# A hybrid DeltaNet and retention layer: blocks 4 and 5 of the MLP made as a pair by seven products, and the opening taken third by third

## The chip, the cores and the metric

The kernel runs on one core of a Trainium2 chip. The metric is the time of one execution on the device, in microseconds. TensorE multiplies, VectorE (DVE in the rows), ScalarE (ACT) and GpSimd (POOL) do the element work, and the queue of SyncE (SP) issues nearly all transfers. TensorE's granted clock is shown as a share of full speed (1.00 is 2.4 GHz, 0.50 is 1.2 GHz).

## The reference

One layer with two mixers beside each other and an MLP, for 128 prompt and 1024 sample tokens that share the weights. What matters here is how the layer begins and its MLP:

```python
D_MODEL = 1024; SEQ = 128; DEC_SEQ = 1024; D_FF = 4 * D_MODEL

def trunk(x, cond, ...):
    mod = jnp.einsum('bd,de->be', jax.nn.silu(cond), w_mod[l]) + b_mod[l]
    sh1, sc1, g1, sh2, sc2, g2 = jnp.split(mod[:, None, :], 6, axis=-1)
    h = layer_norm(x) * (1.0 + sc1) + sh1
    y, sd, sr = mixer(h, ...)
    x = layer_norm(ALPHA * x + g1 * y, ln1_w[l], ln1_b[l])
    h = layer_norm(x) * (1.0 + sc2) + sh2
    f = jnp.einsum('btf,fd->btd', jnp.square(jax.nn.relu(jnp.einsum('btd,df->btf', h, w_ff1[l]) + b_ff1[l])),
                   w_ff2[l]) + b_ff2[l]
    x = layer_norm(ALPHA * x + g2 * f, ln2_w[l], ln2_b[l])
```

Everything is float32.

## The kernel before, in words

The 1152 tokens lie along the free axis, and the 1024 channels on the partitions, in eight pieces k. Each float32 matrix is held as a high part (a cast by ACT, line 160 in `split`) and a low part (what is left, a subtraction by VectorE, line 161), and each product is three matmuls: high by high, low by high, high by low. The modulated, normalised input h stands in three thirds of 384 tokens, `hH[c]` and `hL[c]`.

**The opening.** `run` executes the steps of a string in order; `^n` puts a step n places ahead in the scheduler's priority. In `STA` a step `x` loads 128 tokens, `l` normalises them, `m` makes a part of the modulation vectors, and `gck` (`modulate_x`) makes the unit of third c and piece k: three transposes on TensorE (line 325), the scaling on ACT (line 328) and on VectorE or ACT (lines 333, 338), and the low part on VectorE or POOL (line 342). The first dense product (line 194) reads all eight units of a third.

**The first MLP product** follows a string `FF1`. A step `F` makes one block of 128 rows of f in the ordinary way, three thirds of 24 matmuls with 384 columns (`dense`, line 194), then relu and square on ACT (lines 1159, 1160) and a store of each third to `HR[f]`. Of F0, F1 and F2 only the first third is left here, the others having been made earlier. A step `P` (`pair`, line 1282) makes two blocks at once by seven products of half size, in the order 3, 4, 6, 7, 5, 2, 1. Each (`product`, line 1246) has two halves of 12 matmuls with 288 columns, 168 matmuls for a pair; the weights are combined by POOL (line 1302) and split; the results are added up by ACT (line 1311) and VectorE (line 1308) in two `af` buffers. Blocks 6 to 31 are the pairs P3 to P15, whose rows and sums `pair_out` stores for the second MLP product; that takes them by seven products too, and the six blocks of `HR` ordinarily.

**The operands of the seven products.** Products 2 and 5 need only copies of quarters of h (`gather`, line 1221, on ACT). Products 3, 4, 6, 7 and 1 need differences and sums of quarters. A step `S` (`combination`) makes one of them, in two halves: `combine` (line 1194) loads the two quarters' halves, 576 KB each, from `HX` in DRAM into two of three `af` buffers, adds them on VectorE (line 1200), casts the high part on ACT (line 1202) and makes the low part on VectorE (line 1203). The `Z` step (`gather_plain`) makes the copies and operand 1. What sets the order: the string sets when a step is written; the scheduler orders each engine's queue by it and by its priorities; the `af` buffers, three, set when a load may start. In the queue of SP a load that waits for its buffer holds up what is behind it.

The text names products by their number and the two halves of an operand by their columns. In rows, `sh`, `sl` are the parts of operands 3, 4, 6 and 7, `d` is an accumulator, `wh`, `wl` the parts of a weight, `rl` a third of a block.

Of the kernel before, what the change touches and what calls it, by code (L numbers as in the profile page):

```python
# [12 lines left out]
ALU = mybir.AluOpType  # L13
# [5 lines left out]
NT = 1152  # L19
# [6 lines left out]
CH = 288  # L26
STA = "x0^150 x4^1000 m2 x1^1000 x5^150 x3^50 x2^400 x6^1000 m0^50 l1 x7^50 l0^50 l2^50 x8 l3^150 l4 m3 l5 m1^1000 g01 g00 l7^1000 l6^400 l8 g02 g03 g10 g21 g12^2500 g22^2500 g11^150 g20^1000 g14^400 g13^150 g23 g06^400 g27 g17 g05^2500 g24^6000 g26^50 g15^2500 g25^150 g04 g07^50 g16^150"
RET = "V2 K0 Q0^150 Z0 V0 S0 O0 V1^400 S1^2500 D^150 N0^150 T0 O1^1000 M1 Q1 N1^2500 T1 K1 Z1^50 M2^1000 M3^50 S2 M0^50 O2^2500 V3^150 N2 S3 T2 O3^1000 N3^1000 T3^50"
DEL = "P0 i0 v0^1000 P1^50 m0^2500 G1 i1 G5 v1^150 b0 s0 P2 G6 b1^50 n0 t0^6000 m1 i2^150 v2 s1 P3 i3 n1 b2^1000 t1^2500 m2 G7 v3 s2^50 G0^150 G4 b3^2500 G2 m3 W^1000 n2 t2^150 s3^400 G3^50 n3^400 O^150 R0 t3^50 R1^1000 R2 R3 R4 R5"
OPS = "L0 M0 L1^1000 L2^400 L3^1000 M1 A0^400 A1 M2 B0^150 A2 L4^400 B1 M3 C0 M4 A3 L5 L6^50 B2 C1 M5 L7 L8 A4 M6 B3 C3 M7 C2 A5 B4 A6^400 B5 A7 M8 C4 C5 B6"  # L30
FFS = "F11 F01 A8 B7 B8^2500 F12 F02 C7 F21 C6^150 C8^6000 F22"
FF1 = "F0 S3 F1 S4 F2 S6 F3 S7 F4 F5 Z0 P3 P4 P5 P6 P7 P8 P9 P10 P11 P12 P13 P14 P15"
NEG = -1.0e30
# [47 lines left out]
def layer_kernel(ctx: ExitStack, tc: tile.TileContext, A, O):  # L81
# [202 lines left out]
    with tc.tile_pool(name="start", bufs=1) as st:  # L284
# [16 lines left out]
        p = pss()  # L301
# [891 lines left out]

    def combine(name, q, u, v, op_):

        x, y = (sb(fq, [128, NT], "af", 3).rearrange("p (k c) -> p k c", c=CH) for _ in range(2))
        for z, n in ((x, u), (y, v)):
            i, j = int(n[0]) - 1, TH * (int(n[1]) - 1) + CH * q
            dma(z, HX[512 * i:512 * i + 512, j:j + CH].rearrange("(k p) c -> p k c", p=128))
        V.tensor_tensor(out=x, in0=x, in1=y, op=op_)  # L1200
        hi, lo = (z[:, :, CH * q:CH * q + CH] for z in H[name])
        S.copy(out=hi, in_=x)
        V.tensor_tensor(out=lo, in0=x, in1=hi.bitcast(F32), op=ALU.subtract)
# [20 lines left out]
    def gather_plain():  # L1224

        q11 = gather(new_quarters(fq, "z0"), "11", 0), gather(new_quarters(hpool, "hH0"), "11", 1)
        q22 = gather(new_quarters(hpool, "hL0"), "22", 0), gather(new_quarters(hpool, "hH1"), "22", 1)
        H["2"], H["5"] = q11, q22
        H["1"] = new_quarters(hpool, "hH2"), new_quarters(hpool, "hL1")
        for q in range(2):  # L1230
            combine("1", q, "11", "22", ALU.add)

# [103 lines left out]
    def pair_stage(p):  # L1336
        rows_ = pair(p)
        if p < NP - 1:
            pair_out(*rows_)
        else:  # L1340
            last_pair.append(rows_)
# [214 lines left out]
```

## Time and profile before

| | |
|---|---|
| median of 3 runs | 1589.14 us (1587.22 to 1591.74) |
| the profiled execution | 1597.36 us |
| its span in the trace | 1595.5 us |
| TensorE busy | 1507.1 us, 94% of the span |
| VectorE, ACT, POOL busy | 1057.4, 724.6, 333.4 us |
| mean granted TensorE clock | 0.977 |
| moved by DMA | 247.81 MB |

Times in rows are microseconds from the start of the span; 1.9 us of the profiled execution lie outside it. A matmul's duration in a row overlaps with the next one's, so the cost of a matmul in a stream is the distance between starts. "Idle before" in brackets is how long the engine had stood still ahead of that instruction, and what it waited for last.

### The profile page before, as it was taken

The numbers are of one execution on the slowest core, as the hardware profiler recorded it, in microseconds if no ns is written. First come the engines' busy times: TensorE is split into PE (matmuls) and PEld (weight loads), VectorE is DVE, ScalarE is ACT, GpSimd is POOL, SyncE is SP. The second block draws the span as 40 slices with busy tenths as digits, with TensorE's granted clock in tenths as the row PEclk, the third lists the DMA queues.
The fourth block names the chain that finished last, engine by engine and source line by source line (L and its number), as shares of the span: only waits on it lengthen the run. The fifth ranks groups of instructions, "written<-read, shape, count | busy, mean of one in ns | idle before, by whom it ended". The sixth has DMA issues, their size and how long they took to land.

```text
span 1595.5 us, 26235 instructions
## 1 busy us (share of the span) xinstructions
PE 1507.1 (94%) x9597; PEld 1328.6 (83%) x9597; DVE 1057.4 (66%) x2045; ACT 724.6 (45%) x1562; POOL 333.4 (21%) x328
## 2 busy tenths in 40 slices
PE   4899999899999999999798999999999999999997
PEld 2697676898898989987687999999998788888885
DVE  4415424568795788657894576656666887867887
ACT  4522312564564464352457565445554453443411
POOL 2201021211112022100541035556553000000000
PEclk9799999999999999999898999999999999999998
DMA  9233556332323123454345944443347989878511
GB/s 347 74 82 83 172 157 200 77 78 70 82 49 102 37 58 108 122 163 161 104 152 158 292 154 139 154 155 128 125 139 260 333 281 315 290 237 284 169 54 66
DMA packets 227378, 247.81 MB, mean 155 GB/s; under 512 B 35956, under 2 KB 161889, under 8 KB 227121
## 3 DMA queue, kind: packets, MB, share of 16 engines
q1 hardware_dynamic: 227249, 246.13, 48.5%
q8 instruction: 76, 1.25, 0.3%
q14 instruction: 53, 0.43, 0.1%
HBM read 185.72 MB, written 56.15 MB: 152 GB/s over the span
## 4 chain that ended last, share of the span: by engine, by line
PE 51%; DVE 10%; issue 4%; ACT 3%; DMA 2%; POOL 2%; SPq 0%; DVEq 0%; POOLq 0%; ACTq 0%
PE d L1252 18%; PE m L1416 14%; PE mm L194 7%; PE d L194 3%; PE p L1416 2%; DVE lnst L245 2%; PE c L900 1%; PE c L891 1%; PE c L884 1%; DVE qk L638 1%; PE co L915 1%; PE co L914 1%; DVE wl L161 1%; DVE acc L1491 1%; POOL lnmv L157 1%
## 5 line engine op out<-in xcount | busy, mean ns | idle before, releaser
L194 PE MATMUL mm<-hH,wh 128*128 128x384 f32 x696 | 247.4, 356 | 2.0 <-ACT raw L634 2.0
L194 PE MATMUL mm<-hL,wh 128*128 128x384 f32 x696 | 246.6, 354 | 0.0
L194 PE MATMUL mm<-hH,wl 128*128 128x384 f32 x696 | 245.7, 354 | 0.0
L161 DVE TENSOR_TENSOR wl<-wr,wh 128x512 fp32r<-128x512 f32 (+1 forms) x149 | 126.8, 855 | 118.3 <-ACT wh L160 109.4
L1416 PE MATMUL m<-vh,sh 128*128 128x512 f32 x460 | 180.6, 393 | 3.4 <-DVE af L1308 3.0
L1416 PE MATMUL m<-vl,sh 128*128 128x512 f32 x460 | 179.8, 393 | 1.4 <-DVE vl L161 1.3
L1416 PE MATMUL m<-vh,sl 128*128 128x512 f32 x460 | 179.6, 391 | 0.4 <-DVE sl L161 0.4
L194 PEld LDWEIGHTS mm<-hH,wh 128*128 128x128 f32 x696 | 133.9, 192 | 7.3 <-ACT raw L634 2.2
L194 PEld LDWEIGHTS mm<-hL,wh 128*128 128x128 f32 x696 | 133.5, 192 | 5.5 <-issue 4.1
L194 PEld LDWEIGHTS mm<-hH,wl 128*128 128x128 f32 x696 | 133.4, 192 | 4.9 <-issue 3.7
L160 ACT CAST wh<-wr 128x512 fp32r<-128x512 f32 (+1 forms) x149 | 88.9, 613 | 78.8 <-PE mm L194 52.2
L1252 PE MATMUL d<-sh,wl 128*128 128x288 f32 x416 | 122.9, 295 | 0.5 <-DVE wl L161 0.5
L1252 PE MATMUL d<-sh,wh 128*128 128x288 f32 x416 | 122.7, 295 | 0.6 <-ACT wh L160 0.6
L1252 PE MATMUL d<-sl,wh 128*128 128x288 f32 x416 | 122.6, 295 | 0.0
L160 ACT CAST sh<-ar 128x512 fp32r<-128x512 f32 x103 | 63.8, 619 | 94.1 <-PE m L1416 46.1
L1416 PEld LDWEIGHTS m<-vh,sh 128*128 128x128 f32 x460 | 86.7, 189 | 22.9 <-issue 3.8
L157 POOL TENSOR_TENSOR lnmv<-lnmv,ex 128x1 f32<-128x1 f32 x36 | 22.0, 612 | 396.4 <-DVE lnmv L249 379.4
L1416 PEld LDWEIGHTS m<-vl,sh 128*128 128x128 f32 x460 | 86.5, 188 | 20.9 <-DVE vl L161 2.1
L1416 PEld LDWEIGHTS m<-vh,sl 128*128 128x128 f32 x460 | 86.8, 189 | 19.1 <-DVE sl L161 0.8
L161 DVE TENSOR_TENSOR sl<-ar,sh 128x512 fp32r<-128x512 f32 x103 | 70.7, 688 | 33.6 <-ACT sh L160 27.6
L1252 PE MATMUL d<-hH,wh 128*128 128x288 f32 x312 | 91.5, 294 | 0.0
L160 ACT CAST vh<-br 128x512 fp32r<-128x512 f32 x103 | 63.8, 619 | 48.9 <-DVE br L1380 32.2
(394 smaller groups left out, 3677.1 us busy)
## 6 DMA issues: line engine op xcount, KB each, us to landing
br<-in_w_ff_dram SPq DMA_DIRECT2D x168, 256.0 KB
ar<-HS SPq DMA_DIRECT2D x91, 256.0 KB
HS<-hL SPq DMA_DIRECT2D x65, 256.0 KB
wm<-in_w_mod_dram SPq DMA_DIRECT2D x32, 512.0 KB
wr<-in_w_in_dram SPq DMA_DIRECT2D x56, 256.0 KB
af<-HX SPq DMA_DIRECT2D x20, 576.0 KB
wm<-in_w_mod_dram SPq DMA_DIRECT2D x8, 1024.0 KB
w3h<-in_w_ff_dram SPq DMA_DIRECT2D x13, 512.0 KB
```

Of the source, the lines that this page charges most:

```text
L157: G.tensor_tensor(out=out, in0=in_, in1=ex[:, 0, 0:n], op=ALU.pow)
L160: S.copy(out=pool_hi, in_=src)
L161: V.tensor_tensor(out=pool_lo, in0=src, in1=pool_hi.bitcast(F32), op=ALU.subtract)
L194: T.matmul(p[:, 0:384], x[:, k % 4, :], y[c][:, k, :], start=(k == 0 and a == 0), stop=(k == 7 and a == 2),)
L245: V.bn_stats(out=st[:, j, :], in_=x[:, 512 * j:512 * j + 512])
L638: V.scalar_tensor_tensor(out=y, in0=raw[:, tap:tap + 1156], scalar=vec2[:, 12 * tap + ct:12 * tap + ct + 1], in1=y, op0=ALU.mult, op1=ALU.add,
L884: T.matmul(p[:, 0:128], qk[:, 0, off(n):off(n) + 128], old, start=True, stop=True)
L891: T.matmul(p[:, 0:128], UP[:, m_, 0, :], r, start=True, stop=True)
L900: T.matmul(p[:, 0:128], kt[:, n, :], y2, start=True, stop=True)
L914: T.matmul(p[:, 128:256], qk[:, 1, off(n):off(n) + 128], old, start=True, stop=True)
L1252: T.matmul(p[:, q, :], w[x][:, k, :], hs[y][:, k, CH * q:CH * q + CH], start=(k == 0 and a == 0), stop=(k == 3 and a == 2),)
L1416: T.matmul(p, x[i], w[j], start=(first and a == 0), stop=(last and a == 2))
```

## The change

In the opening, the units of a third are written one after another, those of the first four pieces ahead of those of the last four, and without most priorities. In the first MLP product, F4 and F5 go, and a step P2 comes behind Z: blocks 4 and 5 are made as a pair. P2 does not go through `pair_out`: its two rows are stored whole to `HR[4]` and `HR[5]`, so that the second MLP product finds its six ordinary blocks as before. Operand 1 is no longer loaded into `af` buffers but into the space of `hL2`, the low part of the last third, which is free once its last reader is done.

```diff
--- before.py
+++ after.py
@@ -24,12 +24,12 @@
-STA = "x0^150 x4^1000 m2 x1^1000 x5^150 x3^50 x2^400 x6^1000 m0^50 l1 x7^50 l0^50 l2^50 x8 l3^150 l4 m3 l5 m1^1000 g01 g00 l7^1000 l6^400 l8 g02 g03 g10 g21 g12^2500 g22^2500 g11^150 g20^1000 g14^400 g13^150 g23 g06^400 g27 g17 g05^2500 g24^6000 g26^50 g15^2500 g25^150 g04 g07^50 g16^150"
+STA = "x0^150 x4^1000 m2 x1^1000 x5^150 x3^50 x2^400 x6^1000 m0^50 l1 x7^50 l0^50 l2^50 x8 l3^150 l4 m3 l5 m1^1000 g00 g01 g02 g03 l7^1000 l6^400 l8 g10 g11 g12 g13 g20 g21 g22 g23 g04 g05 g06 g07 g14 g15 g16 g17 g24 g25 g26 g27"
...
-FF1 = "F0 S3 F1 S4 F2 S6 F3 S7 F4 F5 Z0 P3 P4 P5 P6 P7 P8 P9 P10 P11 P12 P13 P14 P15"
+FF1 = "F0 S3 F1 S4 F2 S6 F3 S7 Z0 P2 P3 P4 P5 P6 P7 P8 P9 P10 P11 P12 P13 P14 P15"
...
@@ -1191,9 +1191,9 @@
         c, j = divmod(a + TH * (int(name[1]) - 1), 384)
         return (hL if lo else hH)[c][:, k:k + 4, j:j + n]
-    def combine(name, q, u, v, op_):
-
-        x, y = (sb(fq, [128, NT], "af", 3).rearrange("p (k c) -> p k c", c=CH) for _ in range(2))
+    def combine(name, q, u, v, op_, staging=None):
+
+        x, y = (z.rearrange("p (k c) -> p k c", c=CH) for z in staging or [sb(fq, [128, NT], "af", 3) for _ in range(2)])
         for z, n in ((x, u), (y, v)):
             i, j = int(n[0]) - 1, TH * (int(n[1]) - 1) + CH * q
             dma(z, HX[512 * i:512 * i + 512, j:j + CH].rearrange("(k p) c -> p k c", p=128))
@@ -1227,8 +1227,9 @@
         q22 = gather(new_quarters(hpool, "hL0"), "22", 0), gather(new_quarters(hpool, "hH1"), "22", 1)
         H["2"], H["5"] = q11, q22
         H["1"] = new_quarters(hpool, "hH2"), new_quarters(hpool, "hL1")
+        z = flat(sb(hpool, [128, 8, 384], "hL2", 1))
         for q in range(2):
-            combine("1", q, "11", "22", ALU.add)
+            combine("1", q, "11", "22", ALU.add, [z[:, 0:NT], z[:, NT:2 * NT]])
     def ordinary(f):
         w = early[f] if f in early else ff1_begin(f)
@@ -1335,7 +1336,10 @@
     def pair_stage(p):
         rows_ = pair(p)
-        if p < NP - 1:
+        if p == 2:
+            dma(HR[4], rows_[1])
+            dma(HR[5], rows_[2])
+        elif p < NP - 1:
             pair_out(*rows_)
         else:
             last_pair.append(rows_)
```

From `product` on, the lines of the changed kernel are one higher (line 1252 becomes 1253).

How the instructions move, at three places. The first is TensorE at the end of F3 (`d_9076` is F3's last third). Before, F4 follows:

```order
L194 MATMUL d_9076<-hL2_7720,wh_9012 128x384
L194 MATMUL d_9076<-hH2_7719,wl_9013 128x384
L194 MATMUL d_9133<-hH0_7715,wh_9121 128x384 [waits Activation_49]
L194 MATMUL d_9133<-hL0_7716,wh_9121 128x384
L194 MATMUL d_9133<-hH0_7715,wl_9122 128x384 [waits DVE_49]
```

Now product 3 of P2 follows:

```order
L194 MATMUL d_9076<-hL2_7720,wh_9012 128x384
L194 MATMUL d_9076<-hH2_7719,wl_9013 128x384
L1253 MATMUL d_9156<-sh3_8900,wh_9152 128x288 [waits Activation_49]
L1253 MATMUL d_9156<-sl3_8901,wh_9152 128x288 [waits DVE_49]
L1253 MATMUL d_9156<-sh3_8900,wl_9153 128x288 [waits DVE_49]
```

The 144 matmuls of F4 and F5 between F3 and the first product of a pair are gone; that product waits for ACT (its weight) and VectorE.

The second place is TensorE at operand 7's second half in P2, as it is now (`d_9252` is product 7, `d_9284` product 5, whose operand is copied into the old spaces of `hL0` and `hH1`):

```order
L1253 MATMUL d_9252<-sh7_9105,wl_9249 128x288
L1253 MATMUL d_9252<-sh7_9105,wh_9248 128x288 [waits Activation_49]
L1253 MATMUL d_9284<-hL0_9127,wh_9280 128x288 [waits PE_49,Activation_49]
L1253 MATMUL d_9284<-hH1_9130,wh_9280 128x288
L1253 MATMUL d_9284<-hL0_9127,wl_9281 128x288
L1253 MATMUL d_9284<-hL0_9127,wh_9280 128x288
L1253 MATMUL d_9284<-hH1_9130,wh_9280 128x288
L1253 MATMUL d_9284<-hL0_9127,wl_9281 128x288
L1253 MATMUL d_9284<-hL0_9127,wh_9280 128x288
L1253 MATMUL d_9252<-sl7_9106,wh_9248 128x288 [waits DVE_49]
L1253 MATMUL d_9252<-sh7_9105,wl_9249 128x288
L1253 MATMUL d_9252<-sh7_9105,wh_9248 128x288
```

One matmul of product 7's second half and seven of product 5 stand ahead of the one that reads the second half of `sl7`. Before, the same products of P3 stood behind F5.

The third place is SP's queue with the last loads of the operands. Before (`af_9107` to `af_9115` are operand 7, `af_9333` and on operand 1):

```order
L86 DMA HR4_8514<-rl_9158 128x384 [waits DMAHW4_49,Activation_49]
L86 DMA w3l_9350<-in_w_ff1_dram 128x4x256 [waits PE_49]
L86 DMA af_9108<-HX_7738 128x4x288 [waits DMAHW6_49,DMAHW1_49,DVE_49]
L86 DMA af_9114<-HX_7738 128x4x288 [waits DMAHW7_49,DVE_49]
L86 DMA HR4_8514<-rl_9187 128x384 [waits DMAHW0_49,Activation_49]
L86 DMA HR4_8514<-rl_9216 128x384 [waits Activation_49]
L86 DMA af_9115<-HX_7738 128x4x288 [waits DMAHW6_49,DMAHW2_49,DVE_49]
L86 DMA af_9333<-HX_7738 128x4x288 [waits DMAHW3_49,DVE_49]
L86 DMA HR5_8515<-rl_9257 128x384 [waits DMAHW4_49,Activation_49]
L86 DMA af_9334<-HX_7738 128x4x288 [waits DMAHW5_49,DMAHW2_49,DVE_49]
L86 DMA af_9340<-HX_7738 128x4x288 [waits DVE_49]
L86 DMA HR5_8515<-rl_9286 128x384 [waits DMAHW7_49,Activation_49]
```

Now (`hL2_9135` is operand 1, in the space of `hL2`):

```order
L86 DMA af_8999<-HX_7738 128x4x288 [waits DMAHW5_49,DVE_49]
L86 DMA HR3_8513<-rl_9101 128x384 [waits Activation_49]
L86 DMA af_9000<-HX_7738 128x4x288 [waits DMAHW7_49,DMAHW2_49,DVE_49]
L86 DMA hL2_9135<-HX_7738 128x4x288 [waits DMAHW0_49,PE_49]
L86 DMA af_9107<-HX_7738 128x4x288 [waits DMAHW1_49,DVE_49]
L86 DMA af_9108<-HX_7738 128x4x288 [waits DMAHW7_49,DVE_49]
L86 DMA hL2_9135<-HX_7738 128x4x288 [waits DMAHW3_49]
L86 DMA af_9114<-HX_7738 128x4x288 [waits DMAHW4_49,DVE_49]
L86 DMA af_9115<-HX_7738 128x4x288 [waits DMAHW5_49,DMAHW2_49,DVE_49]
L86 DMA hL2_9135<-HX_7738 128x4x288 [waits DMAHW6_49,DMAHW3_49,DVE_49]
L86 DMA w3h_9389<-in_w_ff1_dram 128x4x256 [waits Pool_49]
L86 DMA hL2_9135<-HX_7738 128x4x288 [waits DMAHW0_49,DVE_49]
```

The stores of F4 and F5 (HR4, HR5) are gone from between the loads, and two of the four loads of operand 1 have moved ahead of operand 7's last ones; the weights of P3, which were issued between them, come behind.

## Rows read from the trace of the kernel before

**Rows 1.** The page's chain of waits by line, share of the span

```profile
PE d L1252 18%; PE m L1416 14%; PE mm L194 7%; PE d L194 3%; PE p L1416 2%; DVE lnst L245 2%; PE c L900 1%; PE c L891 1%; PE c L884 1%; DVE qk L638 1%; PE co L915 1%; PE co L914 1%; DVE wl L161 1%; DVE acc L1491 1%; POOL lnmv L157 1%
```

**Rows 2.** Stretches; columns in the first line

```profile
core 0: us, PE busy (x) PEld busy (x) DVE busy (x) ACT busy (x) POOL busy (x), PEclk, DMA share, GB/s
...
66.40:81.30 14.90, 14.90 (x75) 14.86 (x74) 5.64 (x10) 6.39 (x12) 2.82 (x3) 0.83 0.44 147
...
873.50:900.30 26.80, 26.78 (x145) 26.79 (x146) 12.96 (x12) 14.88 (x22) 0.00 (x0) 0.94 0.90 283
900.30:925.20 24.90, 24.90 (x145) 24.90 (x144) 14.50 (x12) 14.69 (x22) 2.58 (x2) 1.00 0.88 272
925.20:949.20 24.00, 22.81 (x170) 22.35 (x170) 17.66 (x18) 16.00 (x25) 8.15 (x5) 1.00 0.47 145
...
913.00:916.00 3.00, 3.00 (x19) 3.00 (x18) 2.05 (x2) 1.79 (x5) 0.03 (x1) 1.00 1.09 389
```

**Rows 3.** Timeline of VectorE: start us, us, work, count, [idle before]

```profile
881.10 1.36 DVE L1200 TENSOR_TENSOR af<-af 128x1152 f32<-128x1152 f32 x1 [0.36 <-DMA af<-HX]
...
910.62 1.36 DVE L1200 TENSOR_TENSOR af<-af 128x1152 f32<-128x1152 f32 x1 [1.08 <-DMA af<-HX]
...
917.73 1.35 DVE L1200 TENSOR_TENSOR af<-af 128x1152 f32<-128x1152 f32 x1
...
922.94 1.36 DVE L1200 TENSOR_TENSOR af<-af 128x1152 f32<-128x1152 f32 x1 [1.27 <-DMA af<-HX]
...
925.52 1.36 DVE L1203 TENSOR_TENSOR sl<-af,sh 128x1152 fp32r<-128x1152 f32 x1 [1.23 <-ACT sh L1202]
...
934.07 1.90 DVE L1200 TENSOR_TENSOR af<-af 128x1152 f32<-128x1152 f32 x1 [0.68 <-DMA af<-HX]
...
937.20 2.35 DVE L1203 TENSOR_TENSOR hL<-af,hH 128x1152 fp32r<-128x1152 f32 x1
```

**Rows 4.** Timeline of TensorE at P3, P4 and P5

```profile
925.21 0.29 PE L1252 MATMUL d<-sh,wh 128*128 128x288 f32 x1
...
932.38 0.40 PE L1252 MATMUL d<-sh,wh 128*128 128x288 f32 x1 [0.65 <-ACT wh L160]
...
933.44 0.40 PE L1252 MATMUL d<-sh,wl 128*128 128x288 f32 x1 [0.54 <-DVE wl L161]
...
949.19 0.30 PE L1252 MATMUL d<-sh,wh 128*128 128x288 f32 x1
...
971.46 0.29 PE L1252 MATMUL d<-sh,wh 128*128 128x288 f32 x1
```

**Rows 5.** Timeline of SP's queue: a load for a sum

```profile
930.17 0.36 SPq L86 DMA_DIRECT2D af<-HX  x1
```

**Rows 6.** Tile af, seen from SP: who waited, us, times

```profile
  DVE af L1200: 11.1, 9
```

**Rows 7.** Timeline of TensorE after a wait, F3's first matmuls

```profile
873.52 0.67 PE L194 MATMUL d<-hH,wh 128*128 128x384 f32 x1 [3.82 <-ACT tmp L1124]
873.98 0.52 PE L194 MATMUL d<-hL,wh 128*128 128x384 f32 x1
...
876.86 0.41 PE L194 MATMUL d<-hL,wh 128*128 128x384 f32 x1
877.11 0.34 PE L194 MATMUL d<-hH,wl 128*128 128x384 f32 x1
877.29 0.33 PE L194 MATMUL d<-hH,wh 128*128 128x384 f32 x1
```

**Rows 8.** Timeline of ACT, copies of parts

```profile
925.87 1.47 ACT L1221 CAST hL<-hH 128x1536 fp32r<-128x1536 f32 x1
...
927.65 2.20 ACT L1221 CAST hH<-hL 128x768 fp32r<-128x768 f32 x2
```

**Rows 9.** Timeline of TensorE in the opening

```profile
57.47 2.15 PE L325 MATMUL s<-ident,x 128*128 128x128 f32 x9 [1.84 <-DVE tmp L333]
...
62.85 0.48 PE L325 MATMUL s<-ident,x 128*128 128x128 f32 x1 [0.99 <-ACT tmp L338]
...
65.85 0.90 PE L325 MATMUL mm<-ident,x 128*128 128x128 f32 x3 [0.82 <-ACT tmp L338]
66.40 0.67 PE L194 MATMUL mm<-hH,wh 128*128 128x384 f32 x1
```

## The prediction

> **What bounds the kernel now.** I began with the chain of waits, read stage by stage. TensorE holds the end: the largest piece of the chain is the seven-product pairs of the first MLP product, line 1252, with 18% of the span [rows 1]. In the table by stretches the two stretches that hold F3 and then F4 and F5 show TensorE busy without a gap, 26.78 of 26.80 and 24.90 of 24.90 us [rows 2]. So what the change takes out of TensorE there would come off the end, unless something that ran beside it is late. That is the second thing to read. Beside F3, F4 and F5 the DMA engines are busy 0.90 and 0.88 of the time, against 0.47 in the stretch of P3 [rows 2]: they bring the halves of the combined operands. The rows of VectorE show when each half is made [rows 3]. The sums of line 1200 for operands 3, 4, 6 and 7, two halves each, start between 881.10 (the first) and 922.94 (the eighth), seven steps of 5.98 us in the mean, the quickest 5.21 (917.73 to 922.94), the slowest 7.11 (910.62 to 917.73). The last low part of operand 7 is made at 925.52 + 1.36 = 926.88. TensorE starts P3 at 925.21 [rows 4]: the operands are ready just as F4 and F5 end. This is the row on which the prediction rests: F4 and F5 are now the cover under which operands 6 and 7 are made.
>
> **Matmuls removed and added.** F4 and F5 are 144 matmuls of 384 columns, 24.90 / 144 = 0.173 us each [rows 2], 24.9 us. P2 is 7 x 24 = 168 matmuls of 288 columns. From the first matmul of P4 (949.19) to that of P5 (971.46) 168 of them take 22.27 us [rows 4], 0.1326 each. That is 2.6 us less. P3 now has two stalls of 0.65 and 0.54 us for its weights, and lasts 949.19 - 925.21 = 23.98 instead of 22.27, so 1.7 more could go, since weights would be prepared beside P2. With every operand in time P2 would end at 900.3 + 22.3 = 922.6 and P3 at 944.9, 4.3 us before the 949.19 of now.
>
> **What is late instead.** The order of TensorE (second place above) puts one matmul of operand 7's second half and seven of product 5 ahead of the first matmul that reads the low part of that half; all behind it waits. I take the time of that low part as unchanged, 926.88, for three reasons. First, each half takes two of the three af buffers, so a load waits until an earlier half is used up; a load issued at 930.17 [rows 5] is summed at 934.07 [rows 3], 3.9 us later, the sum takes 1.36, and VectorE waited for these loads 11.1 us in nine waits [rows 6]. TensorE is nowhere in that loop, so emptying its queue makes no half earlier. Second, what goes through SP's queue from operand 6's first load on is the same within some per cent: before, up to the last load of operand 7, eight loads of 590 KB, five stores of 197 KB and two weight loads of 524 KB, 6.8 MB; now eight loads, three stores, two of the four staged loads of sum 1, 6.5 MB, and one more weight load ahead. Third, the stretch up to 900.3 keeps its loads of HX, and P2's 1.05 MB of weights replace the four weight loads of 262 KB of F4 and F5.
>
> Behind 926.88 stand 11 matmuls of product 7, the other 17 of product 5, and 24 each of products 2 and 1: 76 x 0.1326 = 10.1 us, to 936.95. TensorE has then stood still. In front of them there are only 92 (72 of products 3, 4 and 6, 13 of 7, 7 of 5), 12.2 us at full clock, between 900.3 and 926.88, so some 14 of these 26.6 us are idle.
>
> What idle does to the clock this kernel shows once here: after 3.82 us without a matmul the next ten stand 0.32 us apart, half speed, and take 876.86 - 873.52 = 3.34 instead of 1.73 us [rows 7], 1.6 us lost. I add 1.6: P2 ends at 938.55.
>
> P3 follows with 22.27 us, since its weights have had time: 960.8, against 949.19, **11.6 us later**. From P4 on TensorE has no gap to take this back (22.27 for 168 matmuls), and the order of every engine is the same to the end.
>
> **Other edits, at nothing.** The copies of parts by ACT (line 1221; 1.47 us for one of 128x1536, 2.20 for two of 128x768 [rows 8]) and the first weight cast of P2 behind them delay product 3 by some 5 us; the cover is the 14 us of idle. If operand 7 came early, this would show as the next wait. Sum 1 loads into hL2's space without waiting for af: its second half is needed 11 + 17 + 24 + 12 matmuls, 8.5 us, and the 1.6 of slow clock after the low part of 7, at 937.0. Through af its low part now ends at 937.20 + 2.35 = 939.55 [rows 3]; so 2.6 us is the bound above, and I take nothing, since these loads no longer wait for a buffer. The two stores of 590 KB to HR4 and HR5 are issued some 4 us behind P2's end, and hold two af buffers for the 3.9 us of a load of that size [rows 3, 5]: free at about 938.6 + 4 + 3.9 = 946.5. P3 then has no accumulator to spare only at its fifth product, 4 x 3.2 = 12.7 us in: covered.
>
> **The opening.** The order of the units changes, not their number. All transposes of all thirds still stand ahead of the first dense matmul on TensorE. I take zero. Below: TensorE's clock is 0.83 in the 14.90 us from 66.40 on [rows 2], 0.34 of it at half speed, so at full clock 2.5 us would go. Above: the longest wait between transposes, 1.84 us [rows 9].
>
> **Sum.** +11.6 us. In the profiled execution's own terms 1597.4 + 11.6 = 1609.0; that execution stands 8.2 us above the median of 1589.14, and the prediction is made from the median: **1600.8 us**. A measurement of this kernel can tell about 0.3%, 4.8 us, from no change. This case's own range: with all seven steps at the quickest pace operand 7 is ready 7 x 5.21 = 36.5 instead of 41.84 after the first, 5.4 us sooner; without the loss of clock 1.6 less; and 2.5 from the opening: 1591.3. Above: two more steps like the slowest, 2.3, sum 1's 2.6, or 1.84 in the opening; two of these at once, 1605.7.
>
> **Rivals.**
> *The loads, not the loop, set the pace (not slower).* The DMA engines' 0.88 speaks for it. Place: the loads for operands 6 and 7. The best three microseconds of now move 389 GB/s [rows 2]; two loads, 1.18 MB, then take 3.0 us, and with the sum a step is 4.4. Seven steps end at 881.10 + 30.8 + 3.94 = 915.8; 10.1, 1.6 and 22.3 behind it give 949.8, 0.6 later: 1589.8. It decides once operand 7 is whole by about 915. Against it: the bytes in the queue stay, the mean of that stretch is 272 GB/s [rows 2], and each load waits for a buffer first. The Trainium skill, "HBM Reference", "Specifications (TRN2)", has a core that streams alone at about 425 GB/s; by that a step would be an estimated 4.1 us and the end some 2 us earlier yet. No stretch of this trace reaches it: 389 GB/s is the best three microseconds. Chance 0.13.
> *All hidden.* A step of 3.8 us or less; -4.3 us, 1584.8. No step is near it. 0.04.
> *The opening gains.* The 2.5 us of clock and the 1.84 + 0.99 + 0.82 us of waits between transposes [rows 9] go: 1600.8 - 6.2 = 1594.6. Against it: the waits are for VectorE's and ACT's work on units, which is as much as before. 0.09.
> *The clock stays low.* All 76 matmuls behind operand 7 at half speed: 10.1 instead of 1.6 us lost, 1609.3. For it: several stops one after another in P2, of which this trace has no example; against it: after 873.52 the matmuls were back at 0.17 us within 3.4 us [rows 7]. The Trainium skill, "TensorE: Matmul & The Clock Gate", "HAM oscillation — how this bites in real kernels", tells of a kernel whose every burst of matmuls after a wait for DMA begins at the low clock. By that each stop within the 76 matmuls would cost once more; no run here shows it yet. 0.08.
> The forecast keeps 0.66.
>
> **How the numbers follow.** The range is the forecast's own, 1591 to 1606, which also takes in the opening's gain; left out are the first two rivals, the last, and a little of the forecast's ends. Faster than 1584.4 needs everything hidden and some gain at the opening: 0.04. Within 0.3%: the first rival, most of the second and a low corner of the forecast: 0.17. Slower: 0.79.
>
> **What would show it.** Right: F3 ends near 900; TensorE shows stops in P2, the longest ahead of operand 7's second half, ended by VectorE's low part (line 1203) near 927; sums of line 1200 some 6 us apart, the eighth near 923; P2 ends near 938 and P4 begins near 961; half clock in parts of P2. Wrong: sums some 4.4 us apart or operand 7 whole by 915; a stop in P3's fifth product for an af buffer; a first dense matmul far from 66.4 [rows 9]; or a difference behind P4, where I see none.

## The result and the profile after

The changed kernel takes **1599.2 us** (median of 13 runs, 1592.85 to 1605.47) against 1589.27 us for the kernel before (median of 13 runs beside them); the ratio is 1.0057, 95% interval 1.0038 to 1.0076. By the ratio, which leaves out one execution of the kernel before that took 3743 us, that is 9.1 us slower. The prediction was 1600.8, with a range of 1591 to 1606.

The profiled execution after took 1600.57 us, with a span of 1598.9 us, close to its median; that of before, 1597.36 us, stood 8.1 above its own. So the two traces differ by only 3.4 us in all, and the stages have to be read one by one. One correction to the words on record: where the title of rows 7 and the expectations speak of "F3's first matmul", they mean the first matmul of the section of F0 to F3 (873.52 before, 859.45 after), which is the first third of F0. It is time zero of the table further down.

The chain of waits of the changed kernel by line, from its page, answers to [rows 1]; loads of `af` and VectorE's sums now stand in it:

```profile
PE d L1253 16%; PE m L1420 14%; PE mm L194 7%; PE p L1420 2%; DMA af<-HX 2%; DVE lnst L245 2%; PE c L900 1%; DMA wor<-in_w_o_dram 1%; PE c L891 1%; POOL hL L1332 1%; DVE qk L638 1%; PE c L884 1%; DVE wl L161 1%; PE co L915 1%; DVE af L1200 1%
```

The stretches of F0 to F3, of P2 up to operand 7, and of the rest of P2 with P3 (columns as in [rows 2]):

```profile
859.40:887.20 27.80, 27.75 (x144) 27.58 (x144) 11.50 (x10) 17.24 (x23) 1.30 (x1) 0.90 0.82 259
887.20:913.50 26.30, 15.72 (x89) 14.05 (x89) 21.41 (x19) 15.45 (x22) 5.48 (x4) 0.86 0.91 288
913.50:947.70 34.20, 34.20 (x251) 34.20 (x250) 19.98 (x26) 17.58 (x27) 10.16 (x8) 0.96 0.25 90
```

TensorE is busy 15.7 of 26.3 us in the second stretch, where it was busy without a gap under F4 and F5, while the DMA engines are as busy as before, 0.91. The sums and the low parts on VectorE, which answer to [rows 3] (line 1200 the sums, the first, the seventh and the eighth of operands 3, 4, 6 and 7, line 1203 the last low part of operand 7):

```profile
867.60 1.35 DVE L1200 TENSOR_TENSOR af<-af 128x1152 f32<-128x1152 f32 x1
...
904.13 1.36 DVE L1200 TENSOR_TENSOR af<-af 128x1152 f32<-128x1152 f32 x1 [0.26 <-DMA af<-HX]
...
909.56 1.35 DVE L1200 TENSOR_TENSOR af<-af 128x1152 f32<-128x1152 f32 x1
...
912.13 1.36 DVE L1203 TENSOR_TENSOR sl<-af,sh 128x1152 fp32r<-128x1152 f32 x1 [0.62 <-ACT sh L1202]
```

The first and the eighth sum are 41.96 us apart, a step of 5.99 us where it was 5.98. And the timeline of TensorE, with each stop of over a microsecond in P2, the end of P2 and the first matmuls of P3 (925.40) and P4 (947.67), answering to [rows 4, 7]:

```profile
859.45 0.69 PE L194 MATMUL d<-hH,wh 128*128 128x384 f32 x1 [3.81 <-ACT tmp L1124]
...
891.52 0.40 PE L1253 MATMUL d<-sh,wh 128*128 128x288 f32 x1 [4.17 <-ACT wh L160]
...
903.33 0.40 PE L1253 MATMUL d<-sl,wh 128*128 128x288 f32 x1 [1.19 <-DVE sl L1203]
...
906.73 0.40 PE L1253 MATMUL d<-sh,wh 128*128 128x288 f32 x1 [1.67 <-ACT sh L1202]
...
908.31 0.40 PE L1253 MATMUL d<-sl,wh 128*128 128x288 f32 x1 [1.18 <-DVE sl L1203]
...
912.15 0.61 PE L1253 MATMUL d<-sh,wh 128*128 128x288 f32 x1 [1.74 <-ACT sh L1202]
...
925.40 0.30 PE L1253 MATMUL d<-sh,wh 128*128 128x288 f32 x1
...
947.67 0.29 PE L1253 MATMUL d<-sh,wh 128*128 128x288 f32 x1
```

From the section's first matmul to P4's first one it is 88.22 us, against 949.19 - 873.52 = 75.67 before: **12.55 us lost** here. From P4's first matmul to the first of the second MLP product it is 267.19 us in both. Two other stretches differ. From the first dense matmul to the section's first one it is 798.7 us against 807.1, in work that both kernels share; the other profiles lie between 796 and 811 there. And the second MLP product, from its first matmul to the start of the last one, takes 371.9 us against 366.9; the pair alone, below, comes back to this.

The opening, on the other hand, gained. TensorE's first dense matmul of the changed kernel came at 60.74, against 66.40 in [rows 9]. ACT's rows show what changed. The shapes 128x128 and 128x256 occur in the first third only (the prompt's tokens and the others are scaled apart). Before, ACT still scaled units of the first third after TensorE had begun:

```profile
66.79 0.67 ACT L328 ACTIVATE hH<-mm,modT 128x384 fp32r<-128x384 f32 x1 [0.43 <-PE mm L325]
67.36 0.80 ACT L328 ACTIVATE hH<-s,modT 128x128 fp32r<-128x128 f32 x2
...
69.07 1.03 ACT L328 ACTIVATE hH<-s,modT 128x256 fp32r<-128x256 f32 x2
```

Now the first third is through at 56.61 + 0.56 = 57.2, and what is left beside the dense matmuls are units of the last third (128x384, line 338):

```profile
53.63 1.04 ACT L328 ACTIVATE hH<-mm,modT 128x256 fp32r<-128x256 f32 x2
...
56.61 0.56 ACT L328 ACTIVATE hH<-s,modT 128x256 fp32r<-128x256 f32 x1
...
61.41 1.31 ACT L338 ACTIVATE tmp<-s,modT 128x384 f32<-128x384 f32 x2
...
63.17 0.67 ACT L338 ACTIVATE tmp<-s,modT 128x384 f32<-128x384 f32 x1
```

Not all of the 5.7 us belong to the change, though. In the same 16 matmuls of the modulation vectors, which both kernels run in the same place, the execution of before had half the speed (columns: start us, us, work, count):

```profile
27.98 3.64 PE L209 MATMUL co<-wm,cs 128*32 128x512 f32 x16
```

and the one of the changed kernel

```profile
27.03 1.92 PE L209 MATMUL co<-wm,cs 128*32 128x512 f32 x16
```

The vectors that the first units wait for were made at 34.23 and at 30.75. From there to the first dense matmul it is 32.2 and 30.0 us.

### The profile page after: what moved, and what is told of

Same layout as the page of the kernel before. It is cut to its first block, busy times and chain, and to the rows that moved or that the text cites. A ratio compares the mean times of both kernels' runs of the same rounds, so it can differ in the third digit from the quotient of the medians.

```text
span 1598.9 us, 26299 instructions
## 1 busy us (share of the span) xinstructions
PE 1503.3 (94%) x9621; PEld 1324.3 (83%) x9621; DVE 1062.9 (66%) x2056; ACT 728.8 (46%) x1565; POOL 341.4 (21%) x333
## 4 chain that ended last, share of the span: by engine, by line
PE 47%; DVE 10%; DMA 6%; issue 5%; ACT 3%; POOL 3%; SPq 1%; DVEq 0%; POOLq 0%; ACTq 0%
PE d L1253 16%; PE m L1420 14%; PE mm L194 7%; PE p L1420 2%; DMA af<-HX 2%; DVE lnst L245 2%; PE c L900 1%; DMA wor<-in_w_o_dram 1%; PE c L891 1%; POOL hL L1332 1%; DVE qk L638 1%; PE c L884 1%; DVE wl L161 1%; PE co L915 1%; DVE af L1200 1%
## 5 line engine op out<-in xcount | busy, mean ns | idle before, releaser
L1253 PE MATMUL d<-sh,wh 128*128 128x288 f32 x448 | 133.6, 298 | 7.6 <-ACT wh L160 4.2
L1253 PE MATMUL d<-sl,wh 128*128 128x288 f32 x448 | 133.4, 298 | 2.4 <-DVE sl L1203 2.4
L1253 PE MATMUL d<-sh,wl 128*128 128x288 f32 x448 | 133.5, 298 | 0.6 <-DVE wl L161 0.6
L1420 PEld LDWEIGHTS m<-vh,sh 128*128 128x128 f32 x460 | 86.6, 188 | 27.1 <-ACT vh L160 9.1
L1253 PE MATMUL d<-hH,wh 128*128 128x288 f32 x336 | 98.8, 295 | 0.0
L1309 DVE TENSOR_TENSOR af<-af,d 128x576 f32<-128x576 f32 x112 | 80.3, 748 | 23.3 <-PE d L1253 23.2
```

Of the source, the lines that this page charges most:

```text
L1253: T.matmul(p[:, q, :], w[x][:, k, :], hs[y][:, k, CH * q:CH * q + CH], start=(k == 0 and a == 0), stop=(k == 3 and a == 2),)
L1309: V.tensor_tensor(out=d, in0=d, in1=m, op=ALU.add if sign > 0 else ALU.subtract)
L1420: T.matmul(p, x[i], w[j], start=(first and a == 0), stop=(last and a == 2))
```

## The experiments

All ratios are to the kernel before, run on the same chip in turn. The marks of each profile, in microseconds; the last three columns count from the section's first matmul:

| run | ratio, 95% interval | first vectors to dense | step of a sum | operand 7 whole | P2 begins | P4 begins |
|---|---|---|---|---|---|---|
| before | | 32.2 | 5.98 | 53.4 | | 75.7 |
| the change | 1.0057 (1.0038 to 1.0076) | 30.0 | 5.99 | 54.0 | 32.1 | 88.2 |
| e1_opening | 0.9984 (0.9960 to 1.0009) | 27.1 | 6.11 | 54.9 | | 77.3 |
| e2_pair | 1.0087 (1.0065 to 1.0110) | 30.1 | 6.10 | 54.9 | 32.2 | 88.7 |
| e3_af4 | 1.0072 (1.0050 to 1.0094) | 28.4 | 4.58 | 44.2 | 47.2 | 95.3 |
| e4_khalf | 1.0056 (1.0035 to 1.0077) | 28.5 | 6.15 | 55.4 | 33.7 | 89.2 |
| e5_weights | 1.0120 (1.0071 to 1.0169) | 27.1 | 5.92 | 52.9 | 43.4 | 94.8 |
| e6_af4_weights | 1.0075 (1.0048 to 1.0102) | 28.4 | 5.19 | 47.8 | 42.1 | 91.3 |
| e7_order | 1.0063 (1.0036 to 1.0090) | 28.4 | 5.14 | 47.0 | 41.3 | 90.0 |
| e8_af4_load | 1.0025 (1.0002 to 1.0049) | 27.1 | 5.41 | 50.6 | 27.7 | 83.6 |
| e9_af4_order | 1.0016 (0.9995 to 1.0038) | 27.1 | 5.51 | 49.6 | 26.5 | 80.6 |
| e10_opening_again | 0.9977 (0.9955 to 0.9998) | 28.4 | 5.92 | 53.7 | | 77.2 |
| e11_shared | 1.0028 (1.0007 to 1.0050) | 27.1 | (other sums) | 35.3 | 27.7 | 84.4 |

### The two halves of the change alone

The kernel before with the changed string `STA` and nothing else:

```diff
-STA = "... g01 g00 l7^1000 l6^400 l8 g02 g03 g10 g21 g12^2500 ... g04 g07^50 g16^150"
+STA = "... g00 g01 g02 g03 l7^1000 l6^400 l8 g10 g11 g12 g13 g20 g21 g22 g23 g04 g05 ... g26 g27"
```

> The kernel before with the new order of the opening alone; F4 and F5 stay. Theory: of the 5.7 us by which the first dense matmul came sooner in the changed kernel's trace (66.40 to 60.74), 3.5 were there already when the first modulation vector was ready (34.23 against 30.75), in work that both kernels share, and belong to that one execution. The order itself gives the rest, 2.2 us, and about 1.3 of slow clock behind it: 3 to 4 us faster than before, ratio near 0.998; from the first modulation vector to the first dense matmul some 30 us (32.2 before). Rival: all of it comes from the order, 6 to 7 us faster, ratio near 0.996. My prediction had nothing here: ratio 1.000.

The changed kernel with the old string:

> The changed kernel with the old order of the opening: the pair P2 and the staging alone. Theory: from F3's first matmul to P4's first 88 us as in the changed kernel (75.7 before), so 12 to 13 us slower than before, ratio 1.008, and this minus the gain of the opening makes up the whole change. Rival: the pair also lengthens the second MLP product (first matmul to the end of the matmuls 371.9 in the changed kernel's trace, 366.9 before), then 16 to 17 us slower, ratio 1.0105, and that stretch is 371 to 372 here too.

Measured: 0.9984 and 1.0087. Their product, 1.0071, lies in the interval of the whole change. The second run takes the pair and the new place of operand 1's loads together; no run has the latter alone. The opening alone was run again beside two later kernels:

> The kernel before with the new opening alone, once more beside these two on their chip: the opening's gain was 0.9984 with an interval from 0.9960 to 1.0009. Theory: 2 to 3.5 us, ratio 0.9978 to 0.9988, and from the first modulation vector to the first dense matmul 27 to 30 us (32.2 and 30.1 with the old order). Rival: no gain at all, 30 to 32 us there. It also says which of the three is fastest: if the pair's full saving came through, the run with the other order is 1 to 3 us faster than this.

That gave 0.9977, its interval just below 1, where that of the first run still holds 1: the opening is worth 2.5 to 3.7 us, about as the two theories had it, and it alone is the fastest kernel of this study. Eleven profiles with the new order show 27.1 to 30.0 us from the first vectors to the first dense matmul, two with the old one 30.1 and 32.2. In the pair's run, P4 begins 88.7 us behind the section's first matmul, as in the change. The rival that the pair also lengthens the second MLP product is not refuted: its mark was 371 to 372 us, and that stretch is 371.2 us with the pair alone. In the four profiles that have the pair with three `af` buffers it is 370.2 to 371.9, in the three without the pair 366.9 to 369.7; with the pair and four buffers it is 367.6 to 370.4. The rows show a difference in what TensorE waits for there. The four with three buffers have stops that casts of weights by ACT end, some 16, 21 and 25 us into the product, which no other profile has (here the change):

```profile
1231.21 0.50 PE L1420 MATMUL m<-vh,sh 128*128 128x512 f32 x1 [1.15 <-ACT vh L160]
...
1235.82 0.50 PE L1420 MATMUL m<-vh,sh 128*128 128x512 f32 x1 [1.24 <-ACT vh L160]
...
1240.09 0.50 PE L1420 MATMUL m<-vh,sh 128*128 128x512 f32 x1 [0.94 <-ACT vh L160]
...
1260.24 0.50 PE L1420 MATMUL m<-vh,sh 128*128 128x512 f32 x1 [3.17 <-ACT vh L160]
```

All stops of this product add up to 6.8 to 8.7 us in these four and to 5.1 to 6.5 in the three without the pair. The difference of the means, 2.7 us for the whole stretch, is an estimate from seven profiles; why these casts come later is open.

### What sets the pace of the operands

Four `af` buffers instead of three in the changed kernel:

```diff
-... sb(fq, [128, NT], "af", 3) ...
+... sb(fq, [128, NT], "af", 4) ...
```

> The changed kernel with four af buffers instead of three. P2's weights are then loaded behind the operands, so its first product may begin later; the sums of line 1200 tell the theories apart. Theory of the prediction (a load waits for a buffer): with one more buffer the first load of a half no longer waits for the half before, and the eight sums, 5.99 us apart now, come 4.5 to 5 us apart; operand 7's last low part about 46 us behind F3's first matmul instead of 54. Rival (the DMA engines' rate, 0.91 busy, sets the pace): still 5.7 to 6 us apart, 53 to 54 us, and the time within 3 us of the changed kernel's.

The sums came 4.58 us apart and operand 7 was whole at 44.2 us: the wait for a buffer was what held the loads. Not all of it is the buffer's, since P2's weights no longer stood between these loads; two runs of the next heading, with the weights in the same place, have 5.92 us with three buffers and 5.19 with four. The first and the eighth sum of that run on VectorE:

```profile
868.48 1.35 DVE L1200 TENSOR_TENSOR af<-af 128x1152 f32<-128x1152 f32 x1
...
900.52 1.36 DVE L1200 TENSOR_TENSOR af<-af 128x1152 f32<-128x1152 f32 x1 [0.76 <-DMA af<-HX]
```

The time did not follow, since the scheduler now put P2's weights behind all operand loads in SP's queue, and TensorE stood still for them (the first two rows are SP's, the last one TensorE's; the weights are the tile w3h):

```profile
893.37 0.36 SPq L86 DMA_DIRECT2D af<-HX  x1
...
897.46 0.64 SPq L86 DMA_DIRECT2D w3h<-in_w_ff_dram  x1
```

```profile
907.48 0.61 PE L1253 MATMUL d<-sh,wh 128*128 128x288 f32 x1 [19.25 <-ACT wh L160]
```

The other theory, that the DMA engines' rate sets the pace, was tried on three buffers with larger pieces: the halves of an operand cut by channels.

```diff
-        x, y = (z.rearrange("p (k c) -> p k c", c=CH) for z in ...)
+        x, y = (z.rearrange("p (k c) -> p k c", c=TH) for z in ...)
...
-            i, j = int(n[0]) - 1, TH * (int(n[1]) - 1) + CH * q
-            dma(z, HX[512 * i:512 * i + 512, j:j + CH].rearrange("(k p) c -> p k c", p=128))
+            i, j = 512 * (int(n[0]) - 1) + 256 * q, TH * (int(n[1]) - 1)
+            dma(z, HX[i:i + 256, j:j + TH].rearrange("(k p) c -> p k c", p=128))
...
-        hi, lo = (z[:, :, CH * q:CH * q + CH] for z in H[name])
+        hi, lo = (z[:, 2 * q:2 * q + 2, :] for z in H[name])
...
-        for q in range(2):
-            for k in range(4):
+        for q, k in [(q, 2 * h + k) for h in range(2) for q in range(2) for k in range(2)]:
```

> The changed kernel with the halves of an operand cut by channels instead of by columns: a load of the same 576 KB then consists of pieces of 2304 bytes instead of 1152, and a product runs the four channel pieces two by two over both column halves. Bytes, buffers and numbers of instructions stay. If the DMA engines' rate sets the pace, larger pieces quicken it: sums 4.5 to 5.3 us apart, the time 4 to 8 us less than the changed kernel's. If it is latency and the wait for a buffer, sums stay 5.7 to 6 us apart and the time within 2 us; each product's first column half is then complete later, which may cost up to 1 us in each of the early products.

Steps of 6.15 us, the ratio that of the change: pieces of twice the size quicken nothing while the loads wait for buffers.

### Weights early, and where the wait goes next

Two runs took P2's weights, and their first two splits, ahead by a new step `W` behind F2; the second of them has four buffers, and a third one also another order of products in P2.

```diff
-FF1 = "F0 S3 F1 S4 F2 S6 F3 S7 Z0 P2 ..."
+FF1 = "F0 S3 F1 S4 F2 W2 S6 F3 S7 Z0 P2 ..."
...
+    def take_weights(p):
+        w1 = pair_weights(p)
+        taken[p] = w1, {"3": w_split(w1[0][:, :, 0:128]), "4": w_split(w1[1][:, :, 128:256])}
```

> The changed kernel with P2's weights split for products 3 and 4 as soon as F2 is done, ahead of ACT's copies, three af buffers as in the change. Theory: P2's first matmul then follows F3 without the 4.2 us of idle, but the end of P2 hangs on operand 7's second half alone, which comes as late as before (54 us behind F3's first matmul; that of F3 is time zero here): P4's first matmul still at 87 to 90 us, the time within 3 us of the changed kernel's. Rival: the wait for the first weight is what costs, P4 at 84 us and 4 us faster.

> The same early weights and four af buffers together. With four buffers the sums came 4.6 us apart, and the 19 us of idle ahead of P2 in that run were the wait for weights that were loaded last. Theory: sums 4.6 to 5 us apart, operand 7's last low part 44 to 47 us behind F3's first matmul, 76 matmuls and P3 behind it: P4's first matmul at 77 to 80 us, against 88.2 in the changed kernel and 75.7 to 77.3 with F4 and F5; 8 to 11 us faster than the changed kernel, ratio to before 0.998 to 1.001. Rival: operand 1, whose loads now stand behind operand 7's in SP's queue, takes its place as the last one, P4 at 82 to 85 us and ratio 1.002 to 1.004.

> As the run with early weights and four buffers, and in P2 alone the products in the order 3, 4, 6, 5, 2, 7, 1, so that 48 matmuls of products 5 and 2, which need copies only, stand ahead of operand 7 instead of behind it. Theory: 52 instead of 76 matmuls or fewer remain behind operand 7's low part, up to 3 us are saved if products 3 and 4 are drained from their accumulators in time: P4's first matmul at 75 to 77 us, ratio to before 0.996 to 0.999. Rival: the accumulators, four in all, are drained only when operand 7's sums free the af buffers; then nothing is saved, P4 at 77 to 80 us.

All three missed their numbers by an edit that did more than it should: the new casts stood ahead of F3's own on ACT and waited for P2's load, so F3 stood still instead (the first row is the run with three buffers, the second the one with four):

```profile
890.06 0.69 PE L194 MATMUL d<-hH,wh 128*128 128x384 f32 x1 [13.47 <-ACT wh L160]
```

```profile
883.94 0.69 PE L194 MATMUL d<-hH,wh 128*128 128x384 f32 x1 [11.60 <-ACT wh L160]
```

They still say two things. Three buffers keep the step near 6 us (5.92) with TensorE idle for 13 us in F3, four bring it to 5.2: once more TensorE is not in that loop. And the run with three buffers, where operand 7 came at 52.9 and P2 only at 43.4, shows nothing on the rival that the wait for the first weight is what costs. The rows of the change speak against that rival: behind the 4.17 us for the weight come four stops of over a microsecond, 5.8 us in all, each ended by a part of operand 6 or 7; an earlier start of P2 would, by these rows, have made them longer. No run has tested it alone.

Mended, with the load behind F2 and the splits behind F3, and four buffers, in the two orders of P2's products:

```diff
+FF1 = "F0 S3 F1 S4 F2 W2 S6 F3 X2 S7 Z0 P2 ..."
...
-        for name in "3467521":
+        for name in ("3465271" if p == 2 else "3467521"):
```

(the last two lines in the second of them only).

> The changed kernel with four af buffers, P2's weights loaded once F2 is done, and split for products 3 and 4 behind F3's own weights, so that F3 does not wait (in the two runs before it waited 12 us). Theory: F3 ends 27.7 us behind its section's first dense matmul as in the changed kernel, P2 starts within 1 us of it, sums 4.6 us apart, operand 7's last low part at 44 to 46 us, P4's first matmul at 76.5 to 79.5, against 88.2 in the changed kernel and 75.7 and 77.3 with F4 and F5; 9 to 12 us faster than the changed kernel, ratio to before 0.997 to 1.000 (the opening's gain in it). Rival: operand 1, loaded last, is the next one late: P4 at 80 to 84, ratio 1.001 to 1.004.

> The run of this call with four buffers and the early load, and in P2 alone the products in the order 3, 4, 6, 5, 2, 7, 1. Theory: products 5 and 2, which need copies only, fill the wait ahead of operand 7: P4's first matmul 1 to 3 us earlier than there, 74.5 to 77 us, ratio to before 0.996 to 0.999. Rival: the four accumulators are drained only when operand 7's sums free the af buffers, so nothing is saved, or operand 1 is the last one in both: the same time within 1 us.

P2 now follows F3 at once, and P4 begins at 83.6 and 80.6: 4.6 and 7.6 us gained on the change, but some 4 short of the two theories (of the 3 us between them 1.2 lie ahead of P2, in the clock of F0 to F3). 83.6 is where the first run's rival had it, but not by operand 1, for which TensorE waits only 0.4 us in that run. Operand 7 was whole at 50.6, not at 44 to 46. The stretch in which the halves are made, in the change (first) and in the mended run:

```profile
864.00:910.00 46.00, 37.16 (x215) 35.93 (x214) 29.33 (x25) 27.54 (x37) 6.78 (x5) 0.95 0.87 274
```

```profile
862.00:905.00 43.00, 35.86 (x209) 34.61 (x208) 29.39 (x24) 26.89 (x37) 9.84 (x5) 0.94 0.95 304
880.00:905.00 25.00, 17.86 (x113) 16.61 (x112) 21.22 (x17) 18.21 (x25) 9.84 (x5) 0.94 0.98 315
```

With four buffers and P2's 1.05 MB of weights ahead of operands 6 and 7 the DMA engines are 0.95 to 0.98 busy, at 304 to 315 GB/s, against 0.87 and 274, and the fifth sum, whose loads stand behind these weights, came 7.3 us after the fourth. But the engines' rate is not what held the end of operand 7. Its last load was issued by 898.29, and the last three sums start without a wait for a load, each right behind other work of VectorE (the first row is SP's with those last loads, the next three are VectorE's, the other two ACT's):

```profile
893.09 5.20 SPq L86 DMA_DIRECT2D af<-HX  x3
```

```profile
899.52 1.34 DVE L1200 TENSOR_TENSOR af<-af 128x1152 f32<-128x1152 f32 x1
...
903.72 1.36 DVE L1203 TENSOR_TENSOR sl<-af,sh 128x1152 fp32r<-128x1152 f32 x1 [0.36 <-ACT sh L1202]
905.00 1.35 DVE L1200 TENSOR_TENSOR af<-af 128x1152 f32<-128x1152 f32 x1
```

```profile
902.02 0.62 ACT L160 CAST wh<-wr 128x512 fp32r<-128x512 f32 x1 [2.32 <-POOL wr L1317]
902.54 1.15 ACT L1202 CAST sh<-af 128x1152 fp32r<-128x1152 f32 x1
```

The seventh sum is done at 900.86. Its cast stands in ACT's queue behind that of a weight which waits for POOL, and begins 1.7 us later; the low part waits for the cast, and the eighth sum comes behind the low part. So the second theory is not shown with four buffers either: what was late at the end is the work on P2's weights, which stands between the sums on VectorE and between the casts on ACT. What TensorE waited for in the mended run was still operand 7, and in the other order the accumulators, the reason that run's rival gave (product 2 waits for ACT to drain product 3 into an `af` buffer), though P4 came 3 us sooner and not within 1 us as it said:

```profile
903.75 0.61 PE L1253 MATMUL d<-sh,wh 128*128 128x288 f32 x1 [4.05 <-ACT sh L1202]
```

```profile
904.78 0.40 PE L1253 MATMUL d<-z,wh 128*128 128x288 f32 x1 [3.77 <-ACT af L1326]
```

### Half the loads

Operands 3, 4, 6 and 7 use each quarter of h twice. The last run loads each once, one channel piece of all four quarters at a time, and makes all four sums from it. It also has four `af` buffers, P2's weights loaded and split behind F3, and two buffers instead of three for the thirds of a block (`rl`):

```diff
-        a = sb(fr, [128, 384], "rl", 3)
+        a = sb(fr, [128, 384], "rl", 2)
...
+        raw = {}
+        for h in range(2):
+            z = sb(fq, [128, NT], "af", 4)
+            dma(z, HX[512 * h + 128 * i:512 * h + 128 * i + 128, :])
+            for j in range(2):
+                raw[f"{h + 1}{j + 1}"] = z[:, TH * j:TH * j + TH]
+        for name, d in (("3", sb(fq, [128, TH], "t3", 1)), ("6", raw["12"]), ("4", raw["11"]), ("7", raw["22"])):
+            u, v, op_ = COMBOS[name]
+            hi, lo = (z[:, i, :] for z in H[name])
+            V.tensor_tensor(out=d, in0=raw[u], in1=raw[v], op=op_)
+            S.copy(out=hi, in_=d)
+            V.tensor_tensor(out=lo, in0=d, in1=hi.bitcast(F32), op=ALU.subtract)
```

> The changed kernel with the sums of operands 3, 4, 6 and 7 made channel piece by channel piece from loads that they share: eight loads of 590 KB (two for a piece: all quarters) instead of sixteen, four af buffers, P2's weights loaded and split early as in the run with four buffers and early load. VectorE, ACT and the products do the same amount of work; the sums are half as wide and twice as many. Theory: the pair lost its saving only because the operands came late, by the buffers first and by the DMA engines' rate next; with half the loads VectorE sets the pace, 16 sums and 16 low parts of 0.7 us, about 25 us, and the four operands are whole 29 to 33 us behind F3's section's first matmul, P2 runs with stops of less than 2 us in all, and P4's first matmul comes at 72.5 to 75.5 us, against 75.7 to 77.3 with F4 and F5; with the opening's gain 4 to 6 us faster than before, ratio 0.9955 to 0.998. Rival: operand 1, still loaded at the end, or VectorE's queue in P2 takes over the wait: P4 at 76 to 80, ratio 0.998 to 1.001.

The operands were whole at 892.52 + 0.75 - 857.97 = 35.3 us, 19 us sooner than in the change, 2 us behind the latest that was expected. And P4 still begins at 84.4, 4 us later than even the rival had it: from P2's first matmul on, 169 matmuls take 33.2 us, where 168 take 22.3 at full clock. The rows of TensorE name what is late now: operand 3's last piece, a weight that ACT casts behind its copies, and operand 1, whose loads must wait until the copies have freed `hL2`; the last row is VectorE's, operands 3 to 7 whole:

```profile
890.04 0.40 PE L1263 MATMUL d<-sl,wh 128*128 128x288 f32 x1 [2.10 <-DVE sl L1227]
...
898.66 0.40 PE L1263 MATMUL d<-sh,wh 128*128 128x288 f32 x1 [1.79 <-ACT wh L160]
...
917.01 0.41 PE L1263 MATMUL d<-hH,wh 128*128 128x288 f32 x1 [3.38 <-ACT hH L1202]
```

```profile
892.52 0.75 DVE L1227 TENSOR_TENSOR sl<-af,sh 128x576 fp32r<-128x576 f32 x1
```

7.8 of the 33.2 us are stops, and some 3 are half clock behind them. So with the operands early, ACT's copies and operand 1 are, as these rows read, enough to take the saving: F4 and F5 covered these as well. A version in which the pair pays was not found; the fastest is the new opening with F4 and F5 kept.

## Why the prediction was right, and where it was off

**The cover was the reason: right.** The step of the sums did not change (5.99 for 5.98) when TensorE's work beside it went; operand 7 was whole 54.0 us behind the section's first matmul instead of 53.4; TensorE's last stop in P2, at 912.15, ended with the high part of operand 7's second half, 1.3 us ahead of its low part. The prediction had named the low part as what ends it; the eight matmuls ahead of the first one that reads it, now at half clock, covered that. From operand 7's low part to the end of P2 the sum had 10.1 + 1.6 = 11.7 us; it was 925.40 - 913.49 = 11.9. P3 took 22.27 as it should. The section lost 12.55 us where 11.6 were forecast; 0.7 of the difference is operand 7, and 0.2 the clock.

**The wait for a buffer as the reason for the pace: right, and shown** by the runs with a fourth buffer (4.58 us; 5.19 for 5.92 with the weights in the same place). The rival, the DMA engines' rate, was wrong for three buffers, as the larger pieces showed. With four it is not shown: the engines were up to 0.98 busy, but the last halves waited for VectorE and ACT. The Trainium skill, "HBM Reference", "Specifications (TRN2)", has about 425 GB/s for a core that streams alone; no stretch here reached it: these engines moved 315 over 25 us at 0.98 busy, and 389 over the best three microseconds of [rows 2].

**Other edits, at nothing: right in the sum.** P2's first matmul came 4.2 us late behind ACT's copies ("some 5" in the prediction), inside the idle time. Operand 1's second half was whole at 920.65, ahead of its matmuls, and P3 ran without a stop, so neither it nor the stores to HR4 and HR5 cost anything.

**The clock.** After the stop of 4.17 us the first matmuls were 0.24 us apart, half speed, as after the 3.82 us in [rows 7]; after the stops of 1.19 and 1.18 us they were at full speed (0.13 us from the second on; a single matmul stands behind the stop of 1.67), and half clock came back at 909.48, ahead of the last stop. So the loss behind operand 7 was about the single one that the sum had. The Trainium skill's account of bursts that each begin at the low clock ("TensorE: Matmul & The Clock Gate", "HAM oscillation — how this bites in real kernels") agrees with what followed the long stop here; the waits of its kernel are longer than the two short ones, behind which no burst began low.

**Behind P4, at nothing: off.** The prediction saw no difference there, since "the order of every engine is the same to the end", and named one as a sign of being wrong. From P4 to the second MLP product there is none (267.19 us in both). In that product there is one: 371.9 us against 366.9 in the two traces, 370.2 to 371.9 with the pair and three buffers against 366.9 to 369.7 without the pair in the other profiles, with stops behind ACT's casts of weights that the kernel before does not have.

**The opening: the step that was off.** The prediction took zero, "the order of the units changes, not their number", because all transposes stand ahead of the first dense matmul. That looked at TensorE's queue alone. What follows a transpose, scaling and low part, need not be done for all thirds: the first dense product needs one third, and in the new order ACT and POOL finish the last third beside it. It is worth 2.5 to 3.7 us (0.9984 and 0.9977). This is read from the rows; no run takes the order and the priorities apart. Part of the gain is the clock behind the start, which the lower bound of the range had named: the first 40 dense matmuls, from the first start to the last, span 9.3 and 9.4 us in the two profiles with the old order, and 7.3 to 8.4 in the eleven with the new one, since the half speed ends sooner. The gain stood among the rivals with 6.2 us and 0.09; of the whole 5.7 us in the two traces, 3.5 were the clock of that one execution.

The sum by the parts as measured: 13.9 us (1.0087) less 2.5 to 3.7 gives 10 to 11; the whole measured 9.1, with an interval from 6 to 12. The forecast of 11.6 was nearly right partly by luck, because the pair cost two more than it said and the opening gave three that it did not see. The pair's section lost 11.4 to 13.1 us against the three profiles with F4 and F5 (75.7, 77.3, 77.2); with the estimate of 2.7 for the second MLP product that makes 14 to 16, against 13.9 with an interval of 3.6 to either side. That this is the missing part is likely, not shown.

## What to carry to other kernels

Work that a faster algorithm removes may be the cover of something else: ahead of such a change, look for the latest instruction that prepares an operand and ask by how much it is late without the cover, and whether the engine that is relieved has any part in that chain. If it has not, the whole saving is lost and the later restart of the clock comes on top. When the first wait is lifted, expect the next one close behind: here buffers, then weight work between the operands' sums and casts, then copies and the last operand each took a good part of the saving. And look past the stage: the engines' queues can come out otherwise in a later one that the edit does not touch.

## What was not expected of the hardware

One and the same stretch of 16 matmuls ran at half speed in one execution and at full speed in another (3.64 and 1.92 us), with the same matmuls ahead of it, and the start of the MLP section lay between 855 and 874 us in the profiles of kernels that differ by less than 4 us up to there: single profiles say nothing on differences of some microseconds, and stages have to be compared from marks within them. And a busy share of 0.91 of the DMA engines was not their limit: with a fourth buffer they went on to 0.98 and 315 GB/s, and even there the last sums did not wait for a load. Pieces of 2304 instead of 1152 bytes brought nothing (6.15 us a step against 5.99).
